# Small products of a layer's second block on halves and quarters of the matrix array, and a block inverse without transposes

## The chip, the cores and the metric

One core of a Trainium2 chip runs the whole program. TensorE (PE in the profile) multiplies matrices; VectorE (DVE), ScalarE (ACT) and GpSimd (POOL) work on vectors, and SyncE (SP) issues most of the transfers. Each engine takes its instructions in an order that is fixed when the program is built, and waits at an instruction until what it needs is there. The metric is the time of one execution on the device, in microseconds (us), less is better. Three timed runs of the kernel before gave a median of 2962.59 us (2961.88 to 2964.16).

## The reference

Two layers follow each other on one sequence of 256 tokens with 2048 channels. The first has a gated linear recurrence, an attention with forgetting and a pooling over windows, and then a feed-forward part. The second, which the change touches, has two mixers side by side, and then a feed-forward part too:

```python
def step(S, inp):                      # rwkv7, 16 heads of 64 channels
    r_t, w_t, k_t, v_t, a_t, b_t = inp
    Sa = jnp.einsum('bhvk,bhk->bhv', S, a_t)
    S = S * w_t[:, :, None, :] + Sa[..., None] * b_t[:, :, None, :] + v_t[..., None] * k_t[:, :, None, :]
    return S, jnp.einsum('bhvk,bhk->bhv', S, r_t)
...
sol = lax.linalg.triangular_solve(L + eye, rhs, left_side=True, lower=True, unit_diagonal=True)   # gated delta net
```

The kernel computes both recurrences in chunks of 128 tokens. Within a chunk this needs the inverse of a 128 x 128 triangular matrix, one for each head and chunk: 32 for rwkv's 16 heads, 16 for the 8 heads of the gated delta net.

## The kernel before

**Streamed products.** Nearly all of the time goes into products with big weights. `weights` (L294) brings 128 x 1024 blocks of weights in by SP, ACT rounds each to a high part (`hi`, L306) and DVE subtracts to get a low part (`lo`); `product` (L311) and `step3` (L353) multiply them with the activations, which are kept as high | low too. In the second block a k-tile is one product of 128 x 512 with `hi` and one of 128 x 256 with `lo`. They write PSUM tiles `ps`.

**The mixers** (`mixers`, L892) alternate with these. In each of four groups the rwkv part handles two pairs of heads and the gated delta net one q/k head with its two value heads. For every pair of heads `rwkv_front` streams r, k and v, and `rwkv_rest` (L999) prepares the chunk matrices: the products of `bt` and `kt` with `ar` (a decayed and r decayed, 256 columns), for each of 2 heads and 2 chunks, into one PSUM tile `pf` for each head and chunk; DVE masks them into `ab` (with what the name `both` holds) and `ak`; then `tok` (token-major v) is multiplied with `ak` in two ways, into one further `pf`. A head's channels are 64 partitions, so the products with `ar` contract over 64 rows of the array, and of the two products with `tok` the second has 64 columns of weights.

**The inverse.** `diagonals` inverts blocks of 16 on DVE, and `merged_inverse` (L1117) takes four problems at a time (12 calls in all) from blocks of 16 to 32, 64 and 128: per level it multiplies the off-diagonal part (`off`) with the inverse so far (`xn`), gets `m`, and multiplies that with the transposed inverse (`xt`), which is then transposed on TensorE to give the next `xn`. These are products of 128 x 128 in fp32, the last level and its transpose on 64 x 64.

**Sigmoids.** `sigmoids` (L961) computes, for 8 blocks of channels, two products of `wa` (tanh(wd) in the first 64 rows, ad in the other 64) with up-projections `up` that hold zeros in the other half, into one `pf`, and ACT takes the sigmoid of each half from there.

**PSUM.** `psx_tile` (L238) hands out the banks outside the streamed products: while the mixers run, first parts (`pf`) have a ring of three and the parts behind the inverse (`pb`) a ring of two:

```python
def psx_tile(self, back=False):
    tag = "pb" if back or self.flip() else "pf"
    return self.psx.tile([P, 2 * S], F32, name=tag, tag=tag, bufs=self.pbufs[tag == "pb"])
```

**The order.** A scheduler sets each engine's order when the program is built, from the priorities in the code: `step` (L932) puts the inverse and what follows it ahead by `back_ahead`, the rest stays where the code has it. The inverse of the last group runs beside `out2_first` (L1389), the products with the first 12 k-tiles of the output weights, where all others run beside r, k, v or q, k, v, z.

A product of fp32 data is recorded as two matmuls in the trace, each with its own load of weights (PEld); a transpose and a streamed product are recorded as one.

Of the kernel before, what the change touches and what calls it, by code (L numbers as in the profile page):

```python
# [15 lines left out]
P = 128  # L16
# [7 lines left out]
# ---------------------------------------------------------------- host layout  # L24
def tiles_of(w, k_tiles, cols):
    """[K, N] columns `cols` (a list of index arrays of 128 or fewer) -> [m, 128, k_tiles * 128]."""
    out = np.zeros((len(cols), P, k_tiles, P), w.dtype)
    v = w.reshape(k_tiles, P, w.shape[1])
    for m, (idx, at) in enumerate(cols):
        out[m][:, :, at] = v[:, :, idx].transpose(1, 0, 2)  # L30
    return out.reshape(len(cols), P, k_tiles * P)
# [17 lines left out]
# k-tiles of the second block's w_out: rwkv and gated delta net heads, the last of both at the end  # L49
# [6 lines left out]
def pack(i):  # L56
# [4 lines left out]
    # block 1: f | q k v per head | (rnn_x, rnn_y) per block | pool | gates  # L61
# [21 lines left out]
    # block 2: lora (wd | ad), gd, mixed (a, a, gd tail, b) | r k v per pair of heads | q k v v z z per q/k head  # L83
# [13 lines left out]
    up = np.zeros((8, P, 4, P), np.float32)  # w_up | a_up | g_up (two row blocks)  # L97
# [16 lines left out]
    # per-channel vectors  # L114
# [37 lines left out]
def constants():  # L152
# [4 lines left out]
    for h in range(8):  # L157
# [14 lines left out]
        ("lev16", lev(16)), ("lev32", lev(32)), ("lev64", lev(64)), ("blk16", same(16).astype(np.float32)),  # L172
        ("id16", np.broadcast_to(np.eye(16).reshape(1, 256), (P, 256))),
    ]

# [6 lines left out]
# ---------------------------------------------------------------- device program  # L182
class Prog:
# [12 lines left out]
    # small wrappers  # L196
# [19 lines left out]
    def table_set(self, ins, name):  # L216
        """load a set of functions behind `ins`"""
# [20 lines left out]
    def psx_tile(self, back=False):  # L238
        """a PSUM bank outside the streamed products: two for first parts, three for the parts behind"""
# [30 lines left out]
    # ------------------------------------------------------------ set up  # L270
# [22 lines left out]
    # ------------------------------------------------------------ streamed products  # L293
    def weights(self, src, nkt):  # L294
        """One [128, nkt * 128] block of weights -> list of (hi, lo) of up to 8 k-tiles each."""
# [15 lines left out]
    def product(self, blocks, rhs):  # L311
        """blocks: list of (dram block, k-tiles); rhs(k) -> [128, 512] (high | low) of k-tile k.
        Returns the PSUM tile: the product is its left half plus its right half."""
# [17 lines left out]
    # ------------------------------------------------------------ side chains, stepped between the streamed products  # L331
# [5 lines left out]
    def tick(self):  # L337
        """let every chain go on that has waited long enough"""
# [14 lines left out]
    def step3(self, ps, h, l, x, k, total):  # L353
        """weights high | low times x high | low, but for low times low"""
# [12 lines left out]
    def join(self, ps, rows=P):  # L367
        """left half + right half of a product"""
# [8 lines left out]
    def split(self, dst, src):  # L377
        """dst [128, 512] (high | low) of src [128, 256]"""
# [3 lines left out]
    # ------------------------------------------------------------ rms norm, its scale put off  # L382
# [3 lines left out]
    def squares(self, x, m, gf=None, apart=False):  # L386
        """sums of squares of x [128, 256], channels tile m"""
# [12 lines left out]
    def scaled_split(self, dst, x, g):  # L400
        """dst = split(x * g)"""
# [19 lines left out]
    # ------------------------------------------------------------ softplus(sign * y) on a few rows  # L421
    def softplus(self, out, y, sign, tmp):
        """max(sign*y, 0) + log1p(exp(-|y|)); log1p(e) = 2 atanh(e / (2 + e))"""
# [18 lines left out]
class Block1(Prog):  # L442
# [29 lines left out]
    def start(self, st):  # L472
        """x in, and the first three products step by step with it"""
# [32 lines left out]
    def scaled(self, ps, o, rows=P):  # L506
        """o = (left + right) * rstd"""
        t = self.join(ps, rows)
        self.mul(o, t, self.rstd[:rows])

    # ---- rg-lru: one block of 128 channels at a time, the square roots of all together
    def lru(self, rh, w1, st):
        keep = self.pool("lru1", 1, st=st, side="right")
        tp = self.pool("lru", 2, st=st, side="right")
        # s8 = 8 * softplus(-lam) = -8 * log_sigmoid(lam)
# [6 lines left out]
        for n in range(8):  # L522
# [23 lines left out]
            # 2 * gelu(y) = y * (1 + tanh(sqrt(2 / pi) * (y + 0.044715 * y^3)))  # L546
# [10 lines left out]
    def lru_chain(self, tp, n, wl, u, s8, ns8, hb, kept):  # L557
# [5 lines left out]
        # r = (1 + tanh((.. + b_rg) / 2)) / 2, so s8 * r = 4 * softplus(-lam) * (1 + tanh)  # L563
# [3 lines left out]
        # a = exp(log_a); 1 - a^2 = tanh(-log_a) * (1 + a^2)  # L567
# [7 lines left out]
        # 2 * i * u  # L575
# [13 lines left out]
    # ---- forgetting attention, one head at a time  # L589
    def attention(self, rh, w1, st):  # L590
# [11 lines left out]
        # -F = cumsum(softplus(-(f + b)))  # L602
# [22 lines left out]
    def attention_chain(self, tp, h, q, k, v, fl, fr):  # L625
# [21 lines left out]
        # transposed: probabilities (three blocks) and v (two)  # L647
# [17 lines left out]
    # ---- multiscale pooling, one group of 256 channels at a time  # L665
# [40 lines left out]
    # ---- gates times branches  # L706
# [23 lines left out]
    # ---- x + merged @ w_out  # L730
# [18 lines left out]
    # ---- x + (silu(h @ gate) * (h @ up)) @ down, the hidden width in two halves  # L749
# [39 lines left out]
class Block2(Block1):  # L789
    # ------------------------------------------------------------ two rms norms on end  # L790
# [41 lines left out]
    def out2_second(self):  # L832
        """the rest of x + y @ w_out"""
# [17 lines left out]
    # ------------------------------------------------------------ the last norm, tokens on partitions  # L851
    def feed_out(self, m):
        if m is None:
            # [tokens, 2 halves of them, channels]
# [29 lines left out]
    # ------------------------------------------------------------ mixers  # L884
# [47 lines left out]
    def step(self, pend, first=False):  # L932
        """the inverse of the newest group, or what follows the inverse of the oldest"""
# [19 lines left out]
    def shifted(self, ps, o, j):  # L953
        """o = (1 - mu) * p + mu * previous token's p, p = rstd * product"""
# [471 lines left out]
```

## Time and profile before

| | |
|---|---|
| median of three runs | 2962.59 us |
| the profiled execution, first to last instruction (span) | 2965.1 us |
| TensorE busy | 99% of the span, 17676 matmuls |
| weight loads (PEld) busy | 86% |
| VectorE, ScalarE busy | 67%, 51% |
| transfers | 515.78 MB, mean 174 GB/s |
| the mixers | from about 1590 to about 2180 us |

The profiled execution's own time is on record as its span alone; it is 2.5 us (0.08%) over the median of the timed runs. Since a matmul is pipelined, its duration in a row is longer than the time by which it holds up the next one: the streamed pair `hi`, `lo` lasts 0.40 and 0.28 us, but the pairs start every 0.35 us. So costs on TensorE are best read from where rows start, and from what lies between two starts of the same kind.

### The profile page before, as it was taken

What the parts mean: (1) busy time and instruction counts of PE and PEld (TensorE: products, weight loads), DVE (VectorE), ACT (ScalarE), POOL (GpSimd) and SP (SyncE); (2) the same over time, 40 slices, a digit from 0 to 9 for tenths busy, and PEclk for the clock granted to TensorE, in tenths of its full rate; (3) what the DMA queues carried; (4) which work ended last, traced back from release to release, by engine and by line L of the source; (5) the groups of instructions that cost most, each with busy time, mean ns of one, the idle gap of its engine ahead of it and who ended that gap; (6) DMA issues with size and microseconds to landing.
All of it is one profiled execution on the core that took longest, in us unless ns stands there. A gap on an engine that the chain in (4) does not pass through costs nothing.

```text
span 2965.1 us, 46400 instructions
## 1 busy us (share of the span) xinstructions
PE 2934.4 (99%) x17676; PEld 2558.7 (86%) x17676; DVE 1988.0 (67%) x3393; ACT 1502.8 (51%) x2448; POOL 21.5 (1%) x88
## 2 busy tenths in 40 slices
PE   8999999999999999999999999999999999999998
PEld 8999988888888888888888878888888888888887
DVE  7855766666766665666667777777776665566655
ACT  6644444444454444444456555555564444444454
POOL 0000000000000000000000000000010000000000
PEclk9999999999999999999999999999999999999999
DMA  6544455555655555555565423233465555655554
GB/s 232 184 152 156 172 186 190 185 189 188 226 186 188 187 172 187 200 188 187 179 203 183 143 86 124 85 127 105 145 204 186 186 182 181 199 188 187 183 173 158
DMA packets 178047, 515.78 MB, mean 174 GB/s; under 512 B 32024, under 2 KB 59040, under 8 KB 177568
## 3 DMA queue, kind: packets, MB, share of 16 engines
q1 hardware_dynamic: 177536, 511.80, 51.2%
q8 instruction: 138, 2.26, 0.3%
q10 hardware_dynamic: 288, 1.02, 0.1%
q14 instruction: 85, 0.70, 0.1%
HBM read 505.66 MB, written 7.09 MB: 173 GB/s over the span
## 4 chain that ended last, share of the span: by engine, by line
PE 94%; DMA 2%; DVE 2%; ACT 1%; issue 1%; ACTq 0%; POOLq 0%; DVEq 0%; SPq 0%
PE ps L225 85%; PE pb L225 5%; PE pf L225 3%; DVE lo L198 1%; DMA raw<-wo 0%; ACT hi L306 0%; PE pf L228 0%; DMA up<-up 0%; PE pb L1153 0%; DMA xs<-xo 0%; DMA cmp<-scs 0%; PE pb L228 0%; DMA par<-par 0%; DMA xo<-xs 0%; ACT sg L222 0%
## 5 line engine op out<-in xcount | busy, mean ns | idle before, releaser
L225 PE MATMUL ps<-h,hi 128*128 128x512 f32 (+1 forms) x5904 | 1824.9, 370 | 1.2 <-DVE xp L198 0.9
L198 DVE TENSOR_TENSOR lo<-raw,hi 128x1024 fp32r<-128x1024 f32 (+2 forms) x1028 | 1156.5, 1125 | 811.4 <-ACT hi L306 806.7
L306 ACT CAST hi<-raw 128x1024 fp32r<-128x1024 f32 (+2 forms) x1028 | 995.8, 969 | 1224.9 <-issue 689.9
L225 PE MATMUL ps<-h,lo 128*128 128x256 f32 x5152 | 1414.5, 283 | 0.6 <-DVE lo L198 0.6
L225 PEld LDWEIGHTS ps<-h,hi 128*128 128x128 f32 x5904 | 1045.1, 189 | 179.1 <-issue 6.0
L225 PEld LDWEIGHTS ps<-h,lo 128*128 128x128 f32 x5152 | 974.5, 189 | 32.5 <-issue 2.7
L225 PE MATMUL ps<-mid,hi 128*128 128x512 f32 (+1 forms) x1452 | 492.0, 388 | 0.0
L225 PE MATMUL ps<-mid,lo 128*128 128x256 f32 x1408 | 385.5, 281 | 0.0
L225 PEld LDWEIGHTS ps<-mid,hi 128*128 128x128 f32 x1452 | 265.7, 188 | 55.6
L225 PEld LDWEIGHTS ps<-mid,lo 128*128 128x128 f32 x1408 | 265.1, 188 | 5.8
L198 DVE TENSOR_TENSOR t<-ps,s 128x256 f32<-128x256 f32 x323 | 134.6, 417 | 0.0
L373 ACT COPY s<-ps 128x256 f32<-128x256 f32 x323 | 117.8, 365 | 0.0
L225 PE MATMUL ps<-merged,hi 128*128 128x512 f32 x256 | 89.4, 397 | 0.0
L225 PE MATMUL ps<-merged,lo 128*128 128x256 f32 x256 | 69.3, 281 | 0.0
L225 PEld LDWEIGHTS ps<-merged,hi 128*128 128x128 f32 x256 | 47.1, 188 | 10.4 <-DVE merged L198 0.2
L225 PE MATMUL ps<-y,hi 128*128 128x512 f32 (+1 forms) x160 | 49.6, 363 | 2.2 <-ACT hi L306 2.2
L225 PEld LDWEIGHTS ps<-merged,lo 128*128 128x128 f32 x256 | 48.4, 189 | 1.5
L225 PE MATMUL ps<-yg,hi 128*128 128x512 f32 (+1 forms) x160 | 48.9, 356 | 0.0
L225 PE MATMUL ps<-ya,hi 128*128 128x512 f32 x128 | 46.3, 394 | 0.0
L225 PE MATMUL ps<-yb,hi 128*128 128x512 f32 x128 | 46.2, 394 | 0.0
L225 PE MATMUL ps<-yc,hi 128*128 128x512 f32 x128 | 46.2, 394 | 0.0
L198 DVE TENSOR_TENSOR t<-ps,xres 128x256 f32<-128x256 f32 x78 | 33.1, 425 | 14.6 <-PE ps L225 7.7
(383 smaller groups left out, 2333.2 us busy)
## 6 DMA issues: line engine op xcount, KB each, us to landing
raw<-wg SPq DMA_DIRECT2D x352, 512.0 KB, 3.6
raw<-w SPq DMA_DIRECT2D x292, 512.0 KB, 3.6
raw<-wd SPq DMA_DIRECT2D x128, 512.0 KB, 3.5
raw<-wbr SPq DMA_DIRECT2D x48, 512.0 KB, 3.5
raw<-wo SPq DMA_DIRECT2D x48, 512.0 KB, 4.5
raw<-wd SPq DMA_DIRECT2D x128, 192.0 KB, 3.0
raw<-wo SPq DMA_DIRECT2D x32, 256.0 KB, 3.2
xin<-x SPq DMA_DIRECT2D x4, 512.0 KB, 6.6
```

What stands on the lines that cost most here:

```text
L198: return (e or self.V).tensor_tensor(out=o, in0=x, in1=y, op=op)
L225: return self.T.matmul(o, lhsT=l, rhs=r, start=start, stop=stop, skip_group_check=True)
L306: self.A.copy(hi, raw)
L373: self.A.copy(s[:rows], ps[:rows, S:])
```

## The change

It has three parts, all in the second block.

- `sigmoids`: the two products of a block use 64 rows each (rows 0 to 63 for one, 64 to 127 for the other) and write two PSUM tiles.
- `rwkv_rest`: the loop over chunks is outside and the one over heads inside, so that the products of the two heads, which use different 64 rows, stand next to each other; four PSUM tiles as before, but two are taken at once. The two kinds of products with `tok` are no longer mixed: first the four with 128 columns of weights, then the four with 64, whose heads write different halves of the partitions.
- `merged_inverse`: up to blocks of 64 it holds only the two 64 x 64 blocks on the diagonal, compact, in `xs` (as transposed, and as is). Each level's 128 x 128 product becomes two of 64 x 64, one for each half of rows and columns. The transposes go: at the start products with a unit matrix give the other form, and in each level a second set of products gives it (in the second level for the first half alone). `xt`, the full result, is put together at the end, its zero block set by POOL. The last level is as before.

```diff
-        ("lev16", lev(16)), ("lev32", lev(32)), ("lev64", lev(64)), ("blk16", same(16).astype(np.float32)),
         ("id16", np.broadcast_to(np.eye(16).reshape(1, 256), (P, 256))),
+        ("id64", np.tile(np.eye(64), (2, 1))),
+        ("lev16c", fold64(lev(16))), ("lev32c", fold64(lev(32))), ("blk16c", fold64(same(16).astype(np.float32))),
     ]
+def fold64(m):
+    return np.concatenate([m[:64, :64], m[64:, 64:]], 0)
...
     def sigmoids(self):
         self.sg = []
         for j in range(8):
             up = self.w(S, "up")
             self.nc.sync.dma_start(out=up, in_=self.a["up2"][j][:, :S])
-            ps = self.psx_tile()
-            self.mm(ps[:, :S], up[:, :P], self.wa)
-            self.mm(ps[:, S:], up[:, P:], self.wa)
+            pw, pa = self.psx_tile(), self.psx_tile()
+            self.mm(pw[:, :S], up[:64, :P], self.wa[:64])
+            self.mm(pa[:, :S], up[64:, P:], self.wa[64:])
             sg = self.yp.tile([P, 2 * S], F32, name=f"sg{j}", tag=f"yg{j}")
-            self.act(sg[:, :S], ps[:, :S], AF.Sigmoid, bias=self.p("w0", j))
-            ins = self.act(sg[:, S:], ps[:, S:], AF.Sigmoid, bias=self.p("a0", j))
+            self.act(sg[:, :S], pw[:, :S], AF.Sigmoid, bias=self.p("w0", j))
+            ins = self.act(sg[:, S:], pa[:, :S], AF.Sigmoid, bias=self.p("a0", j))
             self.sg.append(sg)
...
-        aks = []
+        aks = {}
         m = self.c("atmask")
-        for h in range(2):
-            hp = slice(64 * h, 64 * h + 64)
-            for c in range(2):
-                pa = self.psx_tile()
-                x = ars[c][hp]
-                self.mm(pa[:, :S], bt[hp, c * P:(c + 1) * P], x)
-                self.mm(pa[:, S:], kt[hp, c * P:(c + 1) * P], x)
+        heads = (slice(0, 64), slice(64, P))
+        for c in range(2):
+            sl = slice(c * P, (c + 1) * P)
+            pas = [self.psx_tile() for _ in heads]
+            for pa, hp in zip(pas, heads):
+                self.mm(pa[:, :S], bt[hp, sl], ars[c][hp])
+            for pa, hp in zip(pas, heads):
+                self.mm(pa[:, S:], kt[hp, sl], ars[c][hp])
+            for h, pa in enumerate(pas):
                 pr = 4 * slot + 2 * h + c
                 self.stt(slots["both"][:, pr].rearrange("p a t -> p (a t)"), pa[:, :S], 3e38, m, ALU.min, ALU.mult)
-                ak = self.w(S, "ak")
+                ak = aks[h, c] = self.w(S, "ak")
                 self.stt(ak, pa[:, S:], 3e38, m, ALU.min, ALU.mult)
-                aks.append(ak)
         pz = self.psx_tile()
+        vt = lambda h, c: tok[:, 2 + c, heads[h]]
         for c in range(2):
             for h in range(2):
-                ak = aks[2 * h + c]
-                vt = tok[:, 2 + c, 64 * h:64 * h + 64]
-                self.mm(pz[:, c * P + 64 * h:c * P + 64 * h + 64], ak[:, :P], vt)
-                self.mm(pz[64 * h:64 * h + 64, S + c * P:S + (c + 1) * P], vt, ak[:, P:])
+                self.mm(pz[:, c * P + 64 * h:c * P + 64 * h + 64], aks[h, c][:, :P], vt(h, c))
+        for c in range(2):
+            for h in range(2):
+                self.mm(pz[heads[h], S + c * P:S + (c + 1) * P], vt(h, c), aks[h, c][:, P:])
...
     def merged_inverse(self, slots, half, gdn):
         full, cm, p0 = slots["ab"], slots["cm"], 4 * half
+        lo, hi = slice(0, 64), slice(64, P)
         q4 = lambda z: z.rearrange("p (q t) -> p q t", q=4)
+        bc = lambda z: z.rearrange("p (a t) -> p a t", a=1).to_broadcast([P, 4, 64])
+        beta = lambda q, rows=slice(0, P): self.nbt[rows, q % 2, 2 * gdn + q // 2:2 * gdn + q // 2 + 1]
+        def pairs(out, left, right, rows=(lo, hi)):
+            for q in range(4):
+                for r in rows:
+                    self.mm(out[r, q], left(r, q), right(r, q))
+        new = lambda: self.gp.tile([P, 2, 4, 64], F32, name="xs", tag="xs", bufs=3)
+        x = new()
+        self.mul(x[:, 0].rearrange("p q (b j) -> p q b j", b=4),
+                 cm[:, p0:p0 + 4].rearrange("p q (a j) -> p q a j", a=1).to_broadcast([P, 4, 4, 16]),
+                 self.c("blk16c").rearrange("p (a b j) -> p a b j", a=1, b=4).to_broadcast([P, 4, 4, 16]))
+        px = self.psx_tile(True)
+        pairs(q4(px[:, :S]), lambda r, q: x[r, 0, q], lambda r, q: self.c("id64", r))
+        self.A.copy(x[:, 1], q4(px[:, :S]))
         xt = self.gp.tile([P, 4, P], F32, name="xt", tag="xt", bufs=2)
-        x = self.gp.tile([P, 4, P], F32, name="xn", tag="xn", bufs=2)
-        self.mul(xt.rearrange("p q (b j) -> p q b j", b=8),
-                 cm[:, p0:p0 + 4].rearrange("p q (a j) -> p q a j", a=1).to_broadcast([P, 4, 8, 16]),
-                 self.c("blk16").rearrange("p (a b j) -> p a b j", a=1, b=8).to_broadcast([P, 4, 8, 16]))
-        px = self.psx_tile(True)
-        for q in range(4):
-            self.tr(px[:, q * P:(q + 1) * P], xt[:, q])
-        self.A.copy(x, q4(px))
-        beta = lambda q, rows=slice(0, P): self.nbt[rows, q % 2, 2 * gdn + q // 2:2 * gdn + q // 2 + 1]
-        for lev in ("lev16", "lev32"):
-            off = self.tp.tile([P, 4, P], F32, name="off", tag="w4")
-            self.mul(off, full[:, p0:p0 + 4], self.bc(lev, 4))
+        self.G.memset(xt[hi, :, lo], 0.0)
+        for lev in ("lev16c", "lev32c"):
+            off = self.tp.tile([P, 4, 64], F32, name="off", tag="w4")
+            for r in (lo, hi):
+                self.mul(off[r], full[r, p0:p0 + 4, r],
+                         self.c(lev, r).rearrange("p (a t) -> p a t", a=1).to_broadcast([64, 4, 64]))
             pm = self.psx_tile(True)
-            for q in range(4):
-                self.mm(pm[:, q * P:(q + 1) * P], off[:, q], x[:, q])
-            m1 = self.tp.tile([P, 4, P], F32, name="m1", tag="w4")
-            pt = self.psx_tile(True)
+            pairs(q4(pm[:, :S]), lambda r, q: off[r, q], lambda r, q: x[r, 1, q])
+            m1 = self.tp.tile([P, 4, 64], F32, name="m1", tag="w4")
             if gdn is None:
-                self.add(m1, q4(pm), self.bc("ident", 4))
+                self.add(m1, q4(pm[:, :S]), bc(self.c("id64")))
             else:
                 for q in range(4):
-                    self.act(m1[:, q], pm[:, q * P:(q + 1) * P], AF.Copy, scale=beta(q))
-            for q in range(4):
-                self.mm(pt[:, q * P:(q + 1) * P], m1[:, q], xt[:, q])
+                    self.act(m1[:, q], pm[:, q * 64:(q + 1) * 64], AF.Copy, scale=beta(q))
+            pt = self.psx_tile(True)
+            end = lev == "lev32c"
+            pairs(q4(pt[:, :S]), lambda r, q: m1[r, q], lambda r, q: x[r, 0, q])
+            pairs(q4(pt[:, S:]), lambda r, q: x[r, 0, q], lambda r, q: m1[r, q], (lo,) if end else (lo, hi))
+            y = new()
+            if not end:
+                both, old = pt.rearrange("p (a q t) -> p a q t", a=2, q=4), x
+                if gdn is None:
+                    self.A.copy(y, both)
+                else:
+                    self.add(y, both, old)
+                x = y
+                continue
+            for r in (lo, hi):
+                if gdn is None:
+                    self.A.copy(xt[r, :, r], q4(pt[r, :S]))
+                else:
+                    self.add(xt[r, :, r], q4(pt[r, :S]), x[r, 0])
             if gdn is None:
-                self.A.copy(xt, q4(pt))
+                self.A.copy(y[lo, 1], q4(pt[lo, S:]))
             else:
-                self.add(xt, q4(pt), xt)
-            px = self.psx_tile(True)
-            n = P if lev == "lev16" else 64
-            for q in range(4):
-                self.T.transpose(px[:n, q * n:(q + 1) * n], xt[:n, q, :n], self.c("ident")[:n, :n])
-            self.A.copy(x[:n, :, :n], q4(px[:n, :4 * n]))
-        lo, hi = slice(0, 64), slice(64, P)
+                self.add(y[lo, 1], q4(pt[lo, S:]), x[lo, 1])
...
```

How this moves the work on TensorE is seen at two places. Names are those of the profile: `ps` is a streamed product, `pf` and `pb` the small ones, and behind the arrow stand what moves through the array and what is loaded into it; `x4` is four in a row.

The first place is the front of the first pair of heads, between two stretches of streamed products for r, k and v. TensorE before:

```order
L225 MATMUL pf<-ar_16451,bt 128x256
L225 MATMUL pf<-ar_16451,kt 128x256
L225 MATMUL pf<-ar_16452,bt 128x256
L225 MATMUL pf<-ar_16452,kt 128x256
...
L225 MATMUL pf<-tok,ak 128x64
L225 MATMUL pf<-ak,tok 64x128
...
L225 MATMUL ps<-h,lo 128x256
L225 MATMUL ps<-h,hi 128x512
L225 MATMUL pf<-tok,ak 128x64
L225 MATMUL pf<-ak,tok 64x128
L225 MATMUL ps<-h,lo 128x256
```

The first four rows (the two chunks of the first head) come once more for the second head, and the pair `tok,ak` and `ak,tok` three times before the streamed rows. TensorE now:

```order
L231 MATMUL pf<-ar_16459,bt 128x256 x2
L231 MATMUL pf<-ar_16459,kt 128x256 x2
L231 MATMUL pf<-ar_16460,bt 128x256
L231 MATMUL pf<-ar_16460,kt 128x256
L231 MATMUL pf<-ar_16460,bt 128x256
L231 MATMUL pf<-ar_16460,kt 128x256
L231 MATMUL pf<-tok,ak 128x64 x2
...
L231 MATMUL pf<-tok,ak 128x64
...
L231 MATMUL pf<-tok,ak 128x64
L231 MATMUL pf<-ak,tok 64x128 x4
```

The two heads' products of the first chunk stand in pairs, those of the second chunk one head behind the other, and the four products with 64 columns of weights stand together at the end; five streamed rows lie between the `tok,ak` rows.

The second place is the inverse of the last group (gated delta net), beside the products with the output weights. TensorE before:

```order
L228 MATMUL pb<-cst,xt 128x128
L225 MATMUL ps<-y,hi 128x512
L228 MATMUL pb<-cst,xt 128x128
L225 MATMUL ps<-y,lo 128x256
...
L225 MATMUL pb<-xn,off 128x128 x2
L225 MATMUL ps<-y,lo 128x256
L225 MATMUL pb<-xn,off 128x128
```

TensorE now:

```order
L231 MATMUL pb<-cst,xs 64x64
L231 MATMUL ps<-y,hi 128x512
L231 MATMUL pb<-cst,xs 64x64
L231 MATMUL ps<-y,lo 128x256
...
L231 MATMUL pb<-xs,off 64x64
L231 MATMUL ps<-yg_18213,hi 128x512
L231 MATMUL pb<-xs,off 64x64
L231 MATMUL ps<-yg_18213,lo 128x256
...
L231 MATMUL pb<-m_22617,xs 64x64
L231 MATMUL ps<-y,hi 128x512
```

In both orders the small products of this one inverse alternate with single streamed ones, before as 128 x 128, now as 64 x 64. In the other eleven inverses they stand in groups of four before and of eight to sixteen now. Counted over the whole order, the 60 products of 64 x 64 of an inverse now stand in 7 to 9 separate groups in the first eleven inverses, and in 42 in the last.

## Rows read from the trace of the kernel before

**Rows 1.** The profile's page: each engine's busy time with its share of the span and instructions, the granted clock in 40 slices (9 is 90% or more of full speed), and the chain of work that ended last, by engine.

```profile
PE 2934.4 (99%) x17676; PEld 2558.7 (86%) x17676; DVE 1988.0 (67%) x3393; ACT 1502.8 (51%) x2448; POOL 21.5 (1%) x88
...
PEclk9999999999999999999999999999999999999999
...
PE 94%; DMA 2%; DVE 2%; ACT 1%; issue 1%; ACTq 0%; POOLq 0%; DVEq 0%; SPq 0%
```

**Rows 2.** Busy time of the engines (with their instructions) in the stretch of the mixers, then the granted clock, the share of the transfer engines and GB/s.

```profile
1590.00:2180.00 590.00, 584.67 (x3547) 482.14 (x3546) 450.49 (x1109) 344.51 (x687) 5.71 (x49) 1.00 0.37 122
```

**Rows 3.** Groups of TensorE's instructions by form in that stretch: line, engine, operation, out<-in, rows*columns of the array, moving form, count, then busy us, mean ns of one, and idle time before them with what ended it.

```profile
L225 PE MATMUL pb<-xt,m 128*128 128x128 f32 x192 | 28.0, 279 | 0.0
L225 PE MATMUL pb<-xn,off 128*128 128x128 f32 x192 | 27.2, 282 | 0.0
L225 PE MATMUL pf<-ar,bt 64*128 64x256 f32 x64 | 19.4, 405 | 0.0
L225 PE MATMUL pf<-ak,tok 128*64 128x128 f32 x64 | 13.8, 298 | 0.0
L225 PE MATMUL pf<-wa,up 128*128 128x256 f32 x32 | 7.4, 386 | 1.3 <-ACT sg L222 1.3
```

**Rows 4.** TensorE in order of time, start and length in us: a group of an inverse on the whole array, between streamed products.

```profile
1737.16 0.39 PE L225 MATMUL ps<-h,hi 128*128 128x512 f32 x1
1737.39 1.05 PE L225 MATMUL pb<-xn,off 128*128 128x128 f32 x8
...
1738.40 0.39 PE L225 MATMUL ps<-h,hi 128*128 128x512 f32 x1
```

**Rows 5.** The same view where small products use a quarter of the array (64*64): a group of four and one of eight.

```profile
1718.21 0.40 PE L225 MATMUL ps<-h,hi 128*128 128x512 f32 x1
1718.54 0.41 PE L1153 MATMUL pb<-cst,xt 64*64 64x64 f32 x4
...
1719.10 0.40 PE L225 MATMUL ps<-h,hi 128*128 128x512 f32 x1
...
1719.81 0.39 PE L225 MATMUL ps<-h,hi 128*128 128x512 f32 x1
1720.12 0.68 PE L225 MATMUL pb<-xn,ab 64*64 64x64 f32 x8
...
1720.95 0.39 PE L225 MATMUL ps<-h,hi 128*128 128x512 f32 x1
...
1721.30 0.40 PE L225 MATMUL ps<-h,hi 128*128 128x512 f32 x1
```

**Rows 6.** The same view: products with 64 columns of weights whose heads write different halves of the partitions, next to each other.

```profile
1724.85 0.44 PE L225 MATMUL pb<-ab,u 128*64 128x128 f32 x4
```

**Rows 7.** The same view: the front of the first pair of heads.

```profile
1648.76 0.70 PE L225 MATMUL pf<-ar,bt 64*128 64x256 f32 x2
1649.30 0.59 PE L225 MATMUL pf<-ar,kt 64*128 64x256 f32 x2
1649.73 0.70 PE L225 MATMUL pf<-ar,bt 64*128 64x256 f32 x4
1650.16 0.70 PE L225 MATMUL pf<-ar,kt 64*128 64x256 f32 x4
1650.74 0.70 PE L225 MATMUL pf<-ar,bt 64*128 64x256 f32 x2
...
1651.80 0.43 PE L225 MATMUL pf<-tok,ak 128*128 128x64 f32 x2
1652.16 0.43 PE L225 MATMUL pf<-ak,tok 128*64 128x128 f32 x2
1652.52 0.43 PE L225 MATMUL pf<-tok,ak 128*128 128x64 f32 x2
...
1655.28 0.40 PE L225 MATMUL ps<-h,hi 128*128 128x512 f32 x1
```

**Rows 8.** The same view: the front of the fourth pair of heads, its first product, the one small product of another chain that stands inside it, and the second streamed product behind its last. Besides, 13 streamed products lie between these rows.

```profile
1787.45 0.70 PE L225 MATMUL pf<-ar,bt 64*128 64x256 f32 x2
...
1789.37 0.70 PE L225 MATMUL pb<-sq,cst 128*128 128x256 f32 x2
1790.00 0.70 PE L225 MATMUL pf<-ar,bt 64*128 64x256 f32 x2
...
1797.15 0.40 PE L225 MATMUL ps<-h,hi 128*128 128x512 f32 x1
```

**Rows 9.** VectorE in order of time: the first and the last of the eight masks that empty the four `pf` of that first front.

```profile
1649.93 0.43 DVE L210 SCALAR_TENSOR_TENSOR ab<-pf,cst 128x256 f32<-128x256 f32 x1 [0.78 <-PE pf L225]
...
1652.46 0.41 DVE L210 SCALAR_TENSOR_TENSOR ak<-pf,cst 128x256 f32<-128x256 f32 x1
```

**Rows 10.** TensorE, and then ScalarE, in order of time, about the sigmoids.

```profile
1601.85 2.86 PE L225 MATMUL pf<-wa,up 128*128 128x256 f32 x12
1604.36 0.58 PE L225 MATMUL ps<-h,hi 128*128 128x512 f32 x1
1606.20 4.58 PE L225 MATMUL pf<-wa,up 128*128 128x256 f32 x20 [1.26 <-ACT sg L222]
1610.44 0.47 PE L225 MATMUL ps<-h,lo 128*128 128x256 f32 x1
...
1603.51 0.42 ACT L222 ACTIVATE gd<-gd 128x256 f32<-128x256 f32 x1
...
1605.31 3.02 ACT L222 ACTIVATE sg<-pf,par 128x256 f32<-128x256 f32 x8
```

More of the change, by code (lines that the diff above doesn't have):

```diff
@@ L1157, in merged_inverse @@
         pm = self.psx_tile(True)
         for q in range(4):
-            self.mm(pm[hi, q * 64:(q + 1) * 64], full[lo, p0 + q, hi], x[lo, q, lo])
-        m1 = self.tp.tile([P, 4, P], F32, name="m1", tag="w4")
+            self.mm(pm[hi, q * 64:(q + 1) * 64], full[lo, p0 + q, hi], y[lo, 1, q])
+        m1 = self.tp.tile([P, 4, 64], F32, name="m1", tag="w4")
         if gdn is None:
-            self.A.copy(m1[hi, :, :64], q4(pm[hi, :S]))
+            self.A.copy(m1[hi], q4(pm[hi, :S]))
         else:
@@ L1164, in merged_inverse @@
             for q in range(4):
-                self.act(m1[hi, q, :64], pm[hi, q * 64:(q + 1) * 64], AF.Copy, scale=beta(q, hi))
+                self.act(m1[hi, q], pm[hi, q * 64:(q + 1) * 64], AF.Copy, scale=beta(q, hi))
         for q in range(4):
-            self.mm(pm[lo, S + q * 64:S + (q + 1) * 64], m1[hi, q, :64], xt[hi, q, hi])
+            self.mm(pm[lo, S + q * 64:S + (q + 1) * 64], m1[hi, q], xt[hi, q, hi])
         self.A.copy(xt[lo, :, hi], q4(pm[lo, S:]))
```

## The prediction

> **What bounds the kernel now.** First the page's busy times, the clock and the chain of waits [rows 1]: TensorE is busy for 99% of the span, the clock is granted in full in every slice, and 94% of the chain that ends last is TensorE's own time. Then the stretch of the mixers, which alone holds what is changed [rows 2]: TensorE 584.67 us busy of 590.00, VectorE 450.49 and ScalarE 344.51, GpSimd nearly nothing, transfers at 0.37. So a microsecond counts only if TensorE spends it, in its own products or in a wait. What other engines gain or lose is free as long as TensorE has other work; at a front or at the sigmoids it has little, and there their pace returns.
>
> Then the small products by form [rows 3], to know how many there are, and TensorE in order of time, since with pipelined matmuls only starts tell what a thing costs. A streamed pair starts every 1721.30 − 1720.95 = 0.35 us [rows 5]. From that:
>
> - a group of eight on the whole array costs 1738.40 − 1737.16 − 0.35 = 0.89 us, 0.11 a record [rows 4];
> - on a quarter, four records cost 1719.10 − 1718.21 − 0.35 = 0.54, and eight 1720.95 − 1719.81 − 0.35 = 0.79 [rows 5]. The difference is 0.0625 a record; what is left, 0.54 − 4 × 0.0625 = 0.29, is a fixed price for each stay in the small form, paid in going there and back to streamed products;
> - two column halves overlap: four products `ab,u` last 0.44, two `ak,tok` of one head 0.43 [rows 6, 7]. Two row halves overlap as well: `ar,bt` of the second chunk of head 1 and the first of head 2, four records, start 1650.16 − 1649.73 = 0.43 before the next kind, as long as two records took just before (1649.73 − 1649.30) [rows 7]. There the two write different `pf`.
>
> **The change part by part.** The sum is made on the profiled execution, 2965.1 us of span, and carried over to the median, 2962.59; they differ by 0.08%.
>
> *Fronts.* Before, the first lasts 1655.28 − 1648.76 = 6.52 us with 3 streamed products inside (0.47: a pair is 0.35, the third about a third of one): 6.05 us. The fourth lasts 9.70, less 13 streamed (2.23) and the `sq` group (about 0.43, as two records of 256 columns): 7.0 us [rows 7, 8]. In bare TensorE time the new front needs 0.29 for the form, 2 × 0.43 for `bt` and `kt` of each chunk with the heads overlapped, which is 1.72 for both chunks, 8 × 0.11 = 0.9 for `tok,ak`, and 0.45 for the four `ak,tok` (as `ab,u`) with 0.29 for that form: 3.66 us. But in the new order the heads stand in pairs only in the first chunk; a ring of three `pf` hasn't room for the second head of the other chunk, which needs a bank that two masks empty first. The first mask starts 0.63 after `kt` (1649.93 − 1649.30), itself some 0.5 after the front's begin, and eight take 2.86 (1652.46 − 1649.93 + 0.33), 0.36 each [rows 9]: the bank is free about 1.9 us after the begin. Chunk 2 therefore takes 4 × 0.43 = 1.72 with the heads one behind the other, not 0.86, and TensorE comes to that head at 0.29 + 0.86 + 0.86 = 2.0, just behind the masks: 4.5 us, and with 0.15 of waiting for the last masks 4.65. The gain is 1.4 to 2.4 us for each of eight fronts, up to 3.4 if streamed products fill all waits. I take 2.0: **−16 us**, ends −8 and −24.
>
> *Sigmoids.* Before, from 1601.85 to 1610.44 with about one streamed pair's lesser part inside: 8.36 us [rows 10]. Their 32 records on the whole array, 386 ns each when pipelined [rows 3], become 32 on halves; each block's two products can overlap, so bare TensorE time is cut to about half (16 blocks' halves of 0.43 / 2 [rows 7], 3.4 us). But each now takes a `pf` of its own where two shared one, from the same ring of three. So TensorE may be only three sigmoids ahead, and ScalarE takes 3.02 / 8 = 0.38 for each [rows 10], 16 × 0.38 = 6 us, after its own work that keeps it till 1603.93 and shares of weight rounding in between. The end then comes some 1.5 us later than now. I take **+1.5**, ends −3 and +3.
>
> *Inverses, the first eleven.* Before, in groups: four transposes 0.44, four groups of eight 3.56, four transposes 0.44, the four on a quarter 0.54, and the last level twice 0.79: 6.56 us, all on the path. Now, with the two quarters of the diagonal overlapped as row and column halves each are: 16 records in the time of eight, 0.79; in each level 16 records again (0.79), then 32 (first level) and 24 with half of them lone (second), 1.29 each by 0.0625 × 16 + 0.29; the last level 1.58 as before. That is 0.79 + 2 × 0.79 + 2 × 1.29 + 1.58 = 6.53. So halving the work is spent on the second product and on going in and out of the form. In these eleven there are 84 groups where 77 would do; seven more at 0.29 are 2 us, offset by the shorter chain (no copy of a transpose between levels), so **0 to +2, taken as +1**. Ends without overlap are rival A; the lower end is −6, were the fixed price half of what the two groups show (three such stays in an inverse before, seven now: 4 × 0.145 × 11).
>
> *The last inverse.* It runs beside the output products, one streamed product between any two of its own, so each one pays the fixed price: 40 groups × 0.29, 104 records × 0.0625, less 0.5 for the few neighbours that overlap, and 1.58 for the last level: 11.6 + 6.5 − 0.5 + 1.58 = 19.2 us. Before, products on the whole array went between streamed ones for no price of form: 6.56. **+12.6 us**; if a lone product between streamed ones keeps half of the price hidden, +7; nothing speaks for more than +14.
>
> *Other engines.* Masks and copies of an inverse are half as large, in two pieces where 64 partitions each are meant; GpSimd's zeroing of a part of `xt` finds an engine with 5.71 us of work in 590 [rows 2]; the constants get narrower by 256 columns, a load at the start which falls on the chain's 2% of DMA [rows 1]. At nothing: streamed products cover all of this. Without that cover an inverse's step would wait for such a piece, by half of a mask's 0.36 [rows 9] 0.2 us.
>
> Sum: −16 + 1.5 + 1 + 12.6 = −1 us, so 2961.5 us.
>
> **Rivals.**
>
> *A: quarters don't overlap (slower).* The two products of a pair write the same bank, `lo` to partitions 0 to 63, `hi` to 64 to 127, from different rows of the array. Every overlap in the trace is of columns in one bank, or of rows in two [rows 6, 7]; none is of rows into one bank. If they go one by one, the inverse needs 16 × 0.0625 + 0.29 = 1.29 where I had 0.79, and 2.29 and 1.79 where I had 1.29: 1.29 + 2 × 1.29 + 2.29 + 1.79 + 1.58 = 9.53, so 2.97 more in each of eleven, +33, and 2993 us in all. It decides as soon as a group of sixteen lasts over 1 us. For it speaks the missing row; against it, that the partitions written are apart, as they are in `ab,u`.
>
> The Trainium skill, "TensorEngine Tiling (Array Packing)", Restrictions and Gotchas, says under PSUM pressure that different row tiles can't access one PSUM bank at the same time. By that rule A would come out, at its 2993. Its page "PSUM — Partial Sum Buffer", on bank collisions, counts a collision of two TensorE writes by bank and quadrant of partitions, and by that the pairs may go together. No run here shows either.
>
> *B: the fronts hide all their waits (faster).* In the order streamed rows stand between the `tok,ak` rows of the first front, and ScalarE may empty the sigmoids as fast as today. Then −23, with sigmoids at 0 and the rest as above: −23 + 0 + 1 + 12.6 = −9.4, so about 2953. For it speaks the fourth front, which with 13 streamed products inside has no row with a wait yet still costs 7.0 where 3.66 are needed; against it, the eight masks of 0.36, which are 2.86 us of VectorE at 76% load.
>
> *C: VectorE sets the pace (slower).* Masks bind every front (−1.4 × 8 = −11), and in the inverses each of about six steps, which now come sooner after one another, waits 0.1 us for its copy (+6.6); with +1.5, +1 and +12.6 that is about +11, so 2973. Against it: groups of one inverse are spaced by streamed products that the scheduler puts there.
>
> **How the numbers follow.** The forecast, with terms as taken, gets 0.43, and its own range is 2954 to 2969; A 0.14; B 0.29; C 0.14. What a measurement can tell from no change is about 0.2%, 5.9 us: faster is below 2956.7, slower above 2968.5. B gives faster nearly all of its chance (0.26), and the forecast's lower edge 0.04: 0.30. A and C give slower 0.25, the forecast's upper edge 0.03: 0.28. The range holds the forecast, B, C and a part of A (an overlap that is only partial): 2949 to 2986.
>
> **What would show it.** In the profile after: a group of sixteen `xs,off` or `cst,xs` of 64 x 64 that costs 0.8 over its streamed neighbours shows the overlap, 1.3 shows A. `ar,bt` with both heads next to each other should take 0.43 for four records. Fronts of 4.7 us, with TensorE waiting for VectorE at `pf<-ar`, fit the forecast, 3.7 without a wait is B. The sigmoids should show TensorE waiting for ScalarE at `pf<-wa` and last about 9.9. In the last inverse, each lone product of 64 x 64 should put its streamed neighbour off by some 0.4. The forecast is wrong if the lone ones cost as little there as on the whole array (then about 2949), or if waits appear in the inverses.

## The result, and the profile after

The changed kernel takes 2983.8 us (median of four runs, 2980.86 to 2985.8), the kernel before 2962.65 beside it: ratio 1.0068, 95% interval 1.0055 to 1.008. It is 21 us slower, where no change was forecast. The two profiled executions read below differ by less, 14.0 us of span (2979.1 and 2965.1): that of the changed kernel is the fastest of its four runs, and that of the kernel before is, by its span, longer than each of its timed runs. What is read from these two traces explains the 14, not the whole 21.

The page of the changed kernel, lines that answer to [rows 1]: busy times, the granted clock, the chain by engine.

```profile
PE 2945.6 (99%) x18396; PEld 2555.2 (86%) x18396; DVE 1990.7 (67%) x3425; ACT 1494.0 (50%) x2440; POOL 26.4 (1%) x100
...
PEclk9999999999999999999999999999799999999999
...
PE 95%; DVE 2%; DMA 2%; ACT 1%; issue 1%; ACTq 0%; POOLq 0%; SPq 0%; DVEq 0%
```

TensorE is as busy as before and as much of the chain (95%, where it was 94%). What is new is one digit: the 7 in the row of the clock. Where the time goes is told by two marks on TensorE, the first product with `y` (there the products with the output weights begin) and the first product of the feed-forward part behind it. First both rows of the changed kernel, then both of the kernel before:

```profile
2050.97 0.39 PE L231 MATMUL ps<-y,hi 128*128 128x512 f32 x1
...
2215.28 0.39 PE L231 MATMUL ps<-h,hi 128*128 128x512 f32 x1
```

```profile
2065.39 0.39 PE L225 MATMUL ps<-y,hi 128*128 128x512 f32 x1
...
2202.51 0.47 PE L225 MATMUL ps<-h,hi 128*128 128x512 f32 x1 [0.25 <-DVE xres L198]
```

Up to the output products the changed kernel has won 14.4 us. Between the marks it needs 164.3 us where it was 137.1, and loses 27.2. That is the stretch of the last inverse. Here are pieces of ten us from it, first of the changed kernel, then of the kernel before, with the columns of [rows 2]:

```profile
2110.00:2120.00 10.00, 9.17 (x49) 6.59 (x47) 5.96 (x10) 2.78 (x4) 0.00 (x0) 0.96 0.74 215
2120.00:2130.00 10.00, 10.00 (x32) 5.99 (x31) 2.41 (x5) 0.99 (x2) 0.00 (x0) 0.50 0.34 103
2130.00:2140.00 10.00, 10.00 (x36) 5.89 (x36) 2.46 (x4) 1.97 (x5) 0.00 (x0) 0.50 0.26 92
2140.00:2150.00 10.00, 10.00 (x34) 6.10 (x33) 1.39 (x2) 0.62 (x1) 0.00 (x0) 0.50 0.05 14
2150.00:2160.00 10.00, 10.00 (x42) 6.35 (x42) 2.38 (x4) 1.98 (x5) 0.00 (x0) 0.50 0.28 93
2160.00:2170.00 10.00, 10.00 (x56) 8.15 (x57) 4.90 (x10) 3.34 (x9) 0.00 (x0) 0.82 0.19 56
```

```profile
2130.00:2140.00 10.00, 9.89 (x66) 8.25 (x65) 6.42 (x13) 5.54 (x11) 0.00 (x0) 1.00 0.71 217
2140.00:2150.00 10.00, 9.98 (x68) 8.00 (x68) 6.10 (x11) 4.83 (x13) 0.00 (x0) 1.00 0.41 135
```

TensorE's busy column reads 10.00 of 10.00, and yet the granted clock is 0.50, which is 1.2 GHz, for about 44 us: what is missing from 1.00 in the six rows is 0.04 + 4 × 0.50 + 0.18 = 2.22, of ten us each, so 22.2 us of clock, which is 44.4 us at half speed. Besides the clock's own column the number of matmuls gives it away: 32 to 42 in ten us, where it was 66 and 68. TensorE's busy share tells nothing here, because a matmul at half clock is counted busy for as long as it takes.

TensorE in order of time shows two prices, that of the form and that of the clock. The last inverse begins at full clock (the rows from 2115.91); in the rows behind the first dots the clock is at half:

```profile
2115.91 0.33 PE L231 MATMUL pb<-cst,xs 64*64 64x64 f32 x2 [0.83 <-DVE xs L204]
2116.17 0.50 PE L231 MATMUL ps<-y,hi 128*128 128x512 f32 x1
2116.59 0.33 PE L231 MATMUL pb<-cst,xs 64*64 64x64 f32 x2
2116.85 0.38 PE L231 MATMUL ps<-y,lo 128*128 128x256 f32 x1
2117.16 0.33 PE L231 MATMUL pb<-cst,xs 64*64 64x64 f32 x2
...
2121.91 0.63 PE L231 MATMUL ps<-y,hi 128*128 128x512 f32 x1
...
2122.55 0.63 PE L231 MATMUL ps<-y,hi 128*128 128x512 f32 x1
...
2127.40 0.47 PE L231 MATMUL pb<-xs,off 64*64 64x64 f32 x2
2127.80 0.79 PE L231 MATMUL ps<-yg,hi 128*128 128x512 f32 x1
2128.53 0.47 PE L231 MATMUL pb<-xs,off 64*64 64x64 f32 x2
2128.93 0.58 PE L231 MATMUL ps<-yg,lo 128*128 128x256 f32 x1
2129.44 0.47 PE L231 MATMUL pb<-xs,off 64*64 64x64 f32 x2
```

A lone product is one that stands by itself between two streamed ones; it is recorded as two matmuls. At full clock two lone products with their streamed pair take 2117.16 − 2115.91 = 1.25 us; less the pair's 0.35 that is 0.45 for a lone product. At half clock the pair takes 2122.55 − 2121.91 = 0.64, and the same sequence 2129.44 − 2127.40 = 2.04: 0.70 for a lone product. So each us at half clock in such a sequence costs 1 − 1.25 / 2.04 = 0.39 us.

### The profile page after: what moved, and what is told of

Its sections match the earlier page's. It is cut to its first block, busy times and chain, and to the rows that moved or that the text cites. A ratio compares the mean times of both kernels' runs of the same rounds, so it can differ in the third digit from the quotient of the medians.

```text
span 2979.1 us, 47881 instructions
## 1 busy us (share of the span) xinstructions
PE 2945.6 (99%) x18396; PEld 2555.2 (86%) x18396; DVE 1990.7 (67%) x3425; ACT 1494.0 (50%) x2440; POOL 26.4 (1%) x100
## 4 chain that ended last, share of the span: by engine, by line
PE 95%; DVE 2%; DMA 2%; ACT 1%; issue 1%; ACTq 0%; POOLq 0%; SPq 0%; DVEq 0%
PE ps L231 86%; PE pb L231 5%; PE pf L231 2%; DVE lo L204 1%; PE pf L234 0%; DMA scs<-e 0%; DMA up<-up 0%; DMA cmp<-scs 0%; DMA par<-par 0%; DMA raw<-wo 0%; DMA raw<-wg 0%; ACT hi L312 0%; ACT rs_y L228 0%; DVE e L204 0%; DVE etmp L204 0%
```

## The experiments

Theory 1: products on a quarter of the array, one between any two streamed ones, cost their form each time and bring the clock down. Rivals: the place in the program brings it down whatever stands there; or the clock is a symptom, and small products as such are dear. Ratios are to the kernel before, run beside each. Its median was 2963.8 beside the last inverse grouped, in its old form and alone new, and beside the fronts alone; it was 2964.2 beside the four others.

**The last inverse grouped**, by putting it, and what follows it in its group, further ahead in the order.

```diff
-            with self.tc.high_priority(offset=self.back_ahead):
+            with self.tc.high_priority(offset=260 if g == 3 and not rwkv else self.back_ahead):
```

> The changed kernel, but the last inverse gets a higher priority (260 places ahead where it had 205), so that its 60 products of 64 x 64 stand in 11 groups between streamed ones, not in 42. Theory 1 (lone products on a quarter of the array cost 0.45 us each and bring the clock down): the granted clock stays at 1.00 through the last inverse, the 27 us that the changed kernel loses from the start of the output products to the next feed-forward part go, and the 14 us won before remain: 2949 us (2944 to 2954). Rival 1 (the clock falls for a reason of this place in the program, such as late weights or the earlier start of the output products, whatever the form of the products): the clock still falls to 0.50 for some 40 us, 2966 to 2975 us. Rival 2 (the clock doesn't matter, 64 x 64 products as such are dear here): 2960 to 2970 us.

Measured: 2955.82 us, ratio 0.9974 (0.9964 to 0.9983).

**The last inverse in its old form**, the others new. The lines that choose the form (the old form's code and its constants, left out here, stand beside the new ones):

```diff
-                    xx = self.merged_inverse(slots, j, None if rwkv else g)
+                    inv = self.merged_inverse_old if g == 3 and not rwkv else self.merged_inverse
+                    xx = inv(slots, j, None if rwkv else g)
```

> The changed kernel with the last inverse alone in its old form (whole array, transposes), its products still one between any two streamed ones. Theory 1: lone products on the whole array have no price of form, the clock stays at 1.00, 2948 us (2943 to 2953). Rival 1 (the place brings the clock down): it falls here too, 2966 or more.

Measured: 2953.96 us, ratio 0.9966 (0.9952 to 0.9979). Both lose the whole slowdown, by an order or a form in one place: the rival that blames the place falls. So does the one by which small products as such are dear, since the grouped run has the same 60 products and takes 28 us less than the changed kernel. Neither got as low as expected, by 6 to 7 us. In part that is the clock at other places: in the profile of the grouped run it is 0.83 between 1600 and 1610, at the sigmoids, and dips in the last inverse too; in that of the old form it is 0.83 in four pieces of ten us (from 1600, 1610, 1700 and 2170). That is 10 and 14 us at half speed, by an estimate with the 0.39 from above some 4 and 5 us of time; the rest is open. The clock at the last inverse in these two, in pieces of ten us, grouped and then old form:

```profile
2110.00:2120.00 10.00, 8.39 (x69) 6.39 (x67) 5.85 (x12) 3.70 (x7) 0.00 (x0) 0.89 0.81 229
2120.00:2130.00 10.00, 10.00 (x91) 7.49 (x92) 4.06 (x7) 2.14 (x8) 0.00 (x0) 0.77 0.35 102
2130.00:2140.00 10.00, 10.00 (x64) 7.92 (x62) 6.54 (x14) 4.54 (x10) 0.00 (x0) 1.00 0.43 135
```

```profile
2120.00:2130.00 10.00, 9.21 (x63) 7.80 (x63) 7.13 (x12) 5.93 (x13) 0.00 (x0) 1.00 0.59 204
2130.00:2140.00 10.00, 9.98 (x65) 7.61 (x63) 4.42 (x8) 4.46 (x11) 0.00 (x0) 1.00 0.51 156
```

Grouped, the clock still dips, but for about 7 us (0.11 + 0.23 of ten us are 3.4 us of clock, 6.8 us at half speed). It isn't at 1.00 throughout, as theory 1 said. This dip comes behind a wait, the first row below, and a wait can do it without small products: in the kernel before TensorE is idle for 2.39 us between 2180 and 2190, with streamed products before and behind, and the next row has the clock at 0.83. What the groups add to such a dip no run separates.

```profile
2116.07 0.68 PE L231 MATMUL pb<-cst,xs 64*64 64x64 f32 x16 [1.61 <-DVE xs L204]
```

```profile
2180.00:2190.00 10.00, 7.61 (x60) 7.07 (x59) 7.21 (x14) 6.17 (x14) 3.65 (x5) 1.00 0.66 227
2190.00:2200.00 10.00, 10.00 (x72) 9.79 (x71) 9.86 (x17) 7.35 (x17) 4.94 (x6) 0.83 0.61 193
```

**The last inverse alone new**, all else as before (the choice of the form as above, the other way round).

> The kernel before with the last inverse alone in the new form. Theory 1: the clock falls to 0.50 there for some 40 us, and the time is that of before plus 27 us: 2990 us (2983 to 2995). Rival 1 (earlier parts of the change shift something that brings the clock down): no fall, before plus 12 at most: 2963 to 2975.

Measured: 2995.1 us, ratio 1.0106 (1.009 to 1.0121), plus 31. Without any other part of the change the clock falls just so, and here with no wait before it: the first lone product follows the streamed ones on end, and the clock falls in the same piece of ten us.

```profile
2130.60 0.32 PE L232 MATMUL pb<-cst,xs 64*64 64x64 f32 x2
```

```profile
2130.00:2140.00 10.00, 10.00 (x41) 6.16 (x39) 3.59 (x7) 1.57 (x3) 0.00 (x0) 0.75 0.55 178
2140.00:2150.00 10.00, 10.00 (x37) 5.88 (x38) 3.81 (x7) 2.59 (x6) 0.00 (x0) 0.50 0.14 39
2150.00:2160.00 10.00, 10.00 (x31) 6.11 (x31) 0.69 (x1) 0.00 (x0) 0.00 (x0) 0.50 0.21 66
2160.00:2170.00 10.00, 10.00 (x39) 5.64 (x38) 2.41 (x5) 2.60 (x6) 0.00 (x0) 0.50 0.11 28
2170.00:2180.00 10.00, 10.00 (x41) 7.53 (x42) 2.61 (x5) 1.42 (x5) 0.00 (x0) 0.50 0.26 82
2180.00:2190.00 10.00, 10.00 (x54) 7.99 (x53) 4.75 (x12) 2.87 (x7) 0.00 (x0) 0.86 0.41 121
```

What is missing from 1.00 is 0.25 + 4 × 0.50 + 0.14 = 2.39 of ten us, which is 47.8 us at half speed.

**The last inverse half lone**: as the first edit, with 230 places in place of 260.

> The changed kernel with the last inverse 230 places ahead: 26 groups, some 16 of them lone products in three stretches. Theory 1 (the clock follows how thinly a stretch is filled): the clock falls in shorter stretches, 10 to 25 us in all at 0.50, 2962 to 2972 us. Rival (any lone product on a quarter, once clock is lost, holds it down until the inverse ends): as the changed kernel, 40 us at 0.50, 2978 to 2985. Rival (only 40 in a row do it): no fall, 2957 to 2960.

Measured: 2965.36 us, ratio 1.0004 (0.9994 to 1.0013); single runs from 2960.68 to 2973.21. Two stretches of its profile:

```profile
2120.00:2130.00 10.00, 10.00 (x52) 6.21 (x50) 3.29 (x5) 0.64 (x2) 0.00 (x0) 0.76 0.39 117
2130.00:2140.00 10.00, 10.00 (x53) 6.73 (x53) 3.15 (x6) 1.88 (x6) 0.00 (x0) 0.73 0.25 83
```

That is some 10 us at half clock, in an execution that is among the faster ones (2962.68). The clock differs from run to run: the ten runs go from 2960.68 us at a mean granted clock of 0.998 to 2973.21 at 0.992, nearly in the order of their clocks. The program is the same in all ten, so the clock is no symptom of dear products; it takes time by itself. 0.006 of 2965 us are 18 us of clock, or 36 us at half speed, and with the 0.39 from above that is an estimate of 14 us, where the runs differ by 12.5. With 42 groups (the changed kernel) the mean clock of the runs is 0.989 to 0.991, with 26 groups 0.992 to 0.998, with 11 groups 0.996 to 0.999, and in the kernel before 0.998 to 0.999.

**The fronts alone** (`rwkv_rest` new, all else as before).

> The kernel before with the new fronts of the heads alone. By the trace of the changed kernel, where products of the fronts take 42.3 us of TensorE where they took 52.5: before minus 10, 2952 to 2953 us. Rival (the prediction's term, which the interplay with the other parts has cut): minus 16, 2947. Rival (waits are only handed on to what follows): minus 3 or less, 2959 to 2963.

Measured: 2953.95 us, ratio 0.9966 (0.9954 to 0.9979), minus 9.9, as the trace of the changed kernel said.

**The first eleven inverses alone** (the new form unless the last).

> The kernel before with the first eleven inverses alone in the new form; fronts, sigmoids and the last inverse are old. By the prediction: +1, so 2964 to 2965 us. By the trace of the changed kernel, where TensorE spends 58.4 us on the inverses up to the output products against 63.9: minus 5 to minus 7, 2957 to 2959. Rival (what is won there is given back behind, by waits in the next steps): 2962 to 2964.

Measured: 2961.24 us, ratio 0.9988 (0.9979 to 0.9997), minus 3: between what the trace of the changed kernel promised and the rival by which it is all given back. In the profile the first product with `y` comes 5.8 us earlier than before (2059.63 against 2065.39), so part of what the stretch of the mixers wins is lost behind it; there TensorE waits 1.92 us for VectorE at the last inverse, and the clock is 0.83 in the ten us from 2130.

**The sigmoids alone.**

> The kernel before with the new sigmoids alone. By the prediction +1.5 (ScalarE is the pace); by the traces of the changed kernel and of its first variants +1 to +2: 2964 to 2966 us. Rival (the clock dips in this stretch, as in the two variants of the changed kernel with a milder last inverse): +2 to +4, with a granted clock under 0.95 between 1600 and 1620 us.

Measured: 2966.34 us, ratio 1.0004 (0.9995 to 1.0013): no change that can be told, by medians plus 2. The profile shows the dip of the clock that the expectation had as the rival:

```profile
1600.00:1604.00 4.00, 2.64 (x14) 1.55 (x12) 1.25 (x3) 3.91 (x8) 0.00 (x0) 1.00 0.62 224
1604.00:1608.00 4.00, 3.76 (x12) 2.31 (x13) 1.23 (x1) 2.98 (x7) 0.00 (x0) 0.61 0.05 10
1608.00:1612.00 4.00, 4.00 (x14) 2.74 (x15) 0.00 (x0) 2.94 (x5) 0.20 (x2) 0.50 0.36 127
1612.00:1616.00 4.00, 4.00 (x16) 3.32 (x15) 2.87 (x4) 2.68 (x4) 0.00 (x0) 0.61 0.00 0
```

After a wait of 1.36 us for ScalarE with products on half the array around it, the clock is halved here too, for some 10 us. In the profiled run of the whole changed kernel it isn't, with the same products. Of the five profiles with the new sigmoids four have a dip here, and none of the five with the old ones, whose wait of 1.26 us is nearly as long; whether the wait or the half array does it no run separates. The time goes with it: the three runs of this kernel with a mean clock of 0.999 take 2962.79 to 2964.29 us, as the kernel before does, and the eight with 0.997 or 0.998 take 2965.57 to 2968.88.

**Without the sigmoids and the last inverse** (new fronts and first eleven inverses; sigmoids and last inverse old).

> New fronts and the new form of the first eleven inverses, with sigmoids and the last inverse old. If the parts add: minus 10 (fronts alone, measured) and what the first eleven are worth: 2948 us if that is minus 6, 2954 if nothing. A version that beats both kernels either way.

Measured: 2952.33 us, ratio 0.9955 (0.9942 to 0.9967), 12 us under the kernel before: the best of all, though not to be told from the fronts alone.

The parts add, within the noise of each: −9.9 − 3.0 + 2.1 + 31.3 = +20.5, and the whole was +21.2.

## Why the prediction was wrong

**The last inverse** is the step that failed: "+12.6 us; if a lone product between streamed ones keeps half of the price hidden, +7; nothing speaks for more than +14." It cost 31 alone, and 29.8 in the whole (2983.8 against 2953.96 with the old form in its place). The price of the form was right: 0.45 for a lone product at full clock, where 0.29 + 2 × 0.0625 = 0.415 was reckoned. What was missing is the clock, taken over from [rows 1] as granted in full in every slice, though the change altered just what TensorE does in that stretch. (A 9 there says 90% or more: the kernel before has a dip of its own, the row at 2190 above.) By the 0.39 from above, 44 us at half clock are an estimate of 17 us of loss, and 12.6 + 17 is 30. With that part alone it is 47.8 us and 18.5, so 31.1, where 31.3 were measured. The 27.2 between the marks is less because the kernel before has its wait and its dip in there; with the old form in its place, the stretch between the same marks takes 135.2 us (2054.70 to 2189.85), 29.2 less than in the changed kernel. A row that could have raised the question was there: four records on a quarter, 0.25 us of products in a stay of 0.54 [rows 5], so that with one product between streamed ones most of each stay goes into the change of form.

The measured 2983.8 lies within the stated range (up to 2986). That is luck: the upper part of it was held open for pairs that overlap only in part, and they overlap in full (below, the first eleven).

The Trainium skill, "TensorEngine Tiling (Array Packing)", Tiling Modes, says that a change of the tiling mode drains TensorE; the 0.29 for each stay agrees. The Trainium skill's page "TensorE: Matmul & The Clock Gate", on HAM oscillation (HAM is its name for what grants the clock), tells of a clock that falls in kernels with gaps between their matmuls. The dip of the kernel before, behind 2.39 us of idle time, agrees in kind; in the last inverse the clock fell with a busy share of 10.00 of 10.00, so that there are no such gaps there, or the profile's busy column doesn't show them. Whether it is the change of form or the small part of the array in use that brings the clock down, no run separates; lone products on the whole array in the same place (the old form, above) leave it at 1.00.

**Fronts** were expected at −16 and gave −9.9 alone. The mechanism was right, as the first one shows:

```profile
1645.70 0.79 PE L231 MATMUL pf<-ar,bt 64*128 64x256 f32 x4
1646.24 0.69 PE L231 MATMUL pf<-ar,kt 64*128 64x256 f32 x4
1646.67 0.59 PE L231 MATMUL pf<-ar,bt 64*128 64x256 f32 x2
1647.10 0.59 PE L231 MATMUL pf<-ar,kt 64*128 64x256 f32 x2
1647.67 0.70 PE L231 MATMUL pf<-ar,bt 64*128 64x256 f32 x2
...
1650.59 0.66 PE L231 MATMUL pf<-ak,tok 128*64 128x128 f32 x8
1651.18 0.50 PE L231 MATMUL ps<-h,hi 128*128 128x512 f32 x1
```

Both heads' `kt` of the first chunk take 1646.67 − 1646.24 = 0.43, the second head of chunk 2 begins 0.57 behind the row before it instead of 0.43, as a short wait for its bank would have it; and the whole front, 1651.18 − 1645.70 = 5.48 less five streamed products (0.82), is 4.66, forecast 4.65. But not every front is like the first. Adding up for all 256 records how far each moves the end of TensorE's work, with the delay of a streamed product right behind, the eight fronts took 52.5 us before and 42.3 now: 4.85 to 6.08 each, the dear ones where an inverse cuts in and adds changes of form. With the fronts alone the same sum is 39.3, so −13 in the fronts, of which the time shows 9.9. So about half of the miss is in the size of the fronts, where one clean front was taken for eight; the other 3 us are lost outside the fronts, and no run shows where.

**First eleven inverses**: +1 expected, −3 measured. The sum of a group held: 32 records of a level, between streamed products,

```profile
1726.63 0.40 PE L231 MATMUL ps<-h,hi 128*128 128x512 f32 x1
1726.96 0.68 PE L231 MATMUL pb<-xs,m 64*64 64x64 f32 x16
1727.47 0.63 PE L231 MATMUL pb<-m,xs 64*64 64x64 f32 x16
...
1728.26 0.40 PE L231 MATMUL ps<-h,hi 128*128 128x512 f32 x1
```

cost 1728.26 − 1726.63 − 0.35 = 1.28, forecast 1.29 with overlap and 2.29 without. What failed is the size of the whole: by the count of TensorE's time in the expectation above the eleven take 58.4 us where they took 63.9, and the prediction had them equal but for the stays. Which of its groups was dearer before or is cheaper now, no run separates. **Rival A is refuted**: two products from different rows of the array into different partitions of one bank do go together. The Trainium skill's "TensorEngine Tiling (Array Packing)", PSUM Pressure, doesn't hold here in its general form; the Trainium skill's "PSUM — Partial Sum Buffer", by quadrants, agrees.

**Sigmoids**: +1.5 expected, 0 to 2 measured. The wait for ScalarE stands where it was put, but it grew little (1.60 us in two waits, 1.26 before), and what the runs above lose goes with the clock, which the term didn't have.

Rivals B and C don't describe the result. The time came out on C's side of the forecast, but VectorE's pace wasn't the cause: in the stretch up to the second mark TensorE waits for it at the small products for 4.6 us in all, where it was 1.4.

## What to carry to other kernels

Small forms of the array pay in groups: here sixteen overlapped products in one stay cost 1.28 us and three lone ones 3 × 0.45 = 1.35, so the order decides, and a change of form is to be read against the order of every place where it lands, not only the commonest. Where a change thins out what TensorE does between streamed products, the clock belongs into the sum, with both of its levels; look at the count of matmuls and the granted clock in a stretch, since the busy share stays at 100%. And each part of a change wants a run of its own: here two of four earned 12 us together, and one lost 31.

## What the runs showed of the hardware

That the clock falls to 1.2 GHz while the profile shows TensorE without idle time, for most of the stretch with lone quarter products (44 us), was not expected; the same products in 11 groups leave it down for 7. Nor was it expected that the clock can differ between executions of one program: behind a wait of 1.36 us between products on half the array it fell for 10 us in one execution and not at all in another. Two row halves that write one bank, in different partitions, run at once: 32 records in 1.28 us.
